# Holding early loads behind the first cache-page splits, moving the window-row copies into the mixer, and loading a table from another queue

## The chip, the cores and the metric

The kernel runs on one core of a Trainium2 chip. The core has five engines with instruction streams of their own: TensorE (PE in the profile; its weight loads are PEld), VectorE (DVE), ScalarE (ACT), GpSimd (POOL) and SyncE (SP). Its 16 DMA engines serve queues that SP and POOL issue into. The metric is the device time of one execution in microseconds (us); lower is better.

## The reference

One layer of a decoder trunk, in fp32, for 512 prompt tokens and 8 samples of 4 new tokens each (544 tokens in all), width 1024. Cut to what matters here:

```python
def layer(x, c, conv_prev, attend, w):
    mod = jax.nn.silu(c) @ w['w_ada'] + w['b_ada']          # modulation, 6 x 1024 columns
    sh1, sc1, g1, sh2, sc2, g2 = jnp.split(mod[:, None, :], 6, axis=-1)
    h = rmsnorm(x, w['norm1']) * (1 + sc1) + sh1
    bg, cg, xin, q, kc, vc, ks, vs, kw, vw, nsa_g, merge_g = split_columns(h @ w['w_in'])
    v, conv_new = short_conv(cg * xin, conv_prev, w['w_conv'], w['b_conv'])
    y_a = (bg * v) @ w['w_out_conv']
    ...
    o_b, nsa_state = attend(qh, gates, kvh(kc, vc), kvh(ks, vs), kvh(kw, vw))
    y_b = o_b @ w['w_o_nsa']
    ga, gb = jnp.split(jax.nn.sigmoid(merge_g), 2, axis=-1)
    x = x + g1 * ((ga * y_a + gb * y_b) @ w['w_out'])
    h2 = rmsnorm(x, w['norm2']) * (1 + sc2) + sh2
    x = x + g2 * ((jax.nn.silu(h2 @ w['w_gate']) * (h2 @ w['w_up'])) @ w['w_down'])

def compress(rows, pe, w1, w2):      # rows of the paged cache, for each sample 1024 past tokens
    ...
    return jax.nn.gelu(flat @ w1) @ w2

def nsa_sample(...):
    kc, vc = compress_kv(full_rows(cache_cmp, kv_cmp), pe, w1, w2)
    ...
    win = jnp.concatenate([cache_win, kv_win], axis=1)
    o = attend_block(q, gates, qpos, kc, vc, sel_t[0], sel_t[1], win[:, :, 0], win[:, :, 1], kwpos, slopes)
    return o, (kv_cmp, kv_sel, win[:, s:])      # new_win_sample: 508 old rows moved up by 4, then 4 new
```

So one output, `new_win_sample`, is mostly a shifted copy of an input: for each of the 8 samples rows 4 to 511 of `cache_win` go to rows 0 to 507, 1 MB per sample.

## The kernel before, in words

Every fp32 product is made of three matmuls. `split` (L213) takes a float tile apart into a high part (ACT, `wh`, L219) and a low part (DVE, `wl`, L220); `mm3` (L224 to L226) multiplies high by high, high by low and low by high. Weights come in slabs of 1 MB (`slab`, L207), each a DMA from SP's queue into one of three buffers named `raw`. The tokens stand in two halves of 288 and 256 columns. An accumulator of the linears is called `lin`.

The stages, in time of the profiled execution:

- 0 to 22 us: tables, the first compression weights (`phi_load`, `phi_split`), the first slab of modulation weights; TensorE also runs transposes of an identity matrix (`wake`, L514) that compute nothing.
- to 166 us: 16 units n = 0 to 15 that compress the cached rows of 8 samples (two units for each). `cmp_gather` (L448) issues 8 indirect DMAs from GpSimd, one for each 256 KB page of a sample; `cmp_split` (L470 on ACT, L471 on DVE) splits the pages into `xh` and `xl`; `cmp_M` (L483 to L485) runs 48 matmuls into `phi`. Between the units `mod_slab` (L273, `modp`) multiplies the eight modulation slabs, and the first normalisation of `xT` (the transposed input) is worked out: `square_acc`, the norm, `modulate`.
- to 306 us: key, value and query linears, whose results go to scratch memory (`q_dr`).
- to 543 us: the mixer. `conv_gen(k)` (three linears for each of eight column blocks; every second block loads three slabs `cg`, `xin`, `bg`) is interleaved with `sample_gen(bp)` for four pairs of samples: scores against compressed rows (`sx`, `px`), the choice of blocks (`imp`), then attention over gathered rows (`sraw`) and over the window rows (`wraw`, L899, two 1 MB DMAs from GpSimd), with transposes of the keys into `kt` (L842). The table `tb` (L716, 1 MB) holds distances and masks for it.
- to 1342 us: the convolution's output linear, prompt attention, output projection, FFN.

The order on each engine is set by a list scheduler of the tile framework, which works with estimated times, so that an instruction can stand far from where it is written. `tc.issue_after(ins)` keeps what is issued inside it behind `ins` on the engine of `ins`. `win_shift` is written in the FFN's loop, but its DMAs read an input and write an output and wait for nothing; the scheduler placed all eight much earlier, at 20.8, 87.1, 109.8, 143.6, 187.2, 220.5, 282.6 and 313.8 us on SP's queue. The loop it is written in:

```python
    for c2 in range(1, FC // 2):
        sg, su = slab("fg", c2), slab("fu", c2)
        if c2 <= DEC_B:
            win_shift(c2 - 1)
```

Of the kernel before, what the change touches and what calls it, by code (L numbers as in the profile page):

```python
# [9 lines left out]
F32 = mybir.dt.float32  # L10
F32R = mybir.dt.float32r
I32 = mybir.dt.int32
AF = mybir.ActivationFunctionType
# [6 lines left out]
KC = 8  # L20
# [5 lines left out]
DEC_B = 8  # L26
# [116 lines left out]
def build(tc, a, o):  # L143
# [58 lines left out]
    def raw_tile(n):  # L202
        return wpool.tile([128, 2048], F32, tag="raw", bufs=3, name=nm(n))

    last_slab = [None]

    def slab(*key):  # L207
        nk, ncol = len(SLABS[key][1]), len(SLABS[key][2])
        v = raw_tile("raw")[:, 0:nk * ncol]
        last_slab[0] = sync.dma_start(v, a["wt"][SLAB_AT[key], :, 0:nk * ncol])  # L210
        return v.rearrange("p (k f) -> p k f", k=nk)

# [49 lines left out]
    cT = cst.tile([128, 8, 32], F32, name="cT")  # L262
    pool.memset(cT, 0.0)

    last_m4 = [None]

    def mod_slab(s, v=None):
        v = slab("ada", s) if v is None else v
        p = tp_ps(nm("modp"))
        for k in range(KC):  # L270
            for hh in range(2):
                j = (k % 2) * 2 + hh
                pe.matmul(p[32 * j:32 * j + 32, 0:128], lhsT=cT[:, k, :], rhs=v[:, k, hh * 128:(hh + 1) * 128], start=(k < 2), stop=(k >= 6))  # L273
        m4 = wpool.tile([128, 128], F32, tag="m4", bufs=2, name=nm("m4"))
        last_m4[0] = act.activation(m4, p[:, 0:128], AF.Copy)
        if modp:
            modp.pop()()
        modp.append(lambda: mod_fin(s, m4))
# [178 lines left out]
    act.activation(cT[:, :, 0:9], c_in.rearrange("p (k n) -> p k n", k=8), AF.Silu)  # L457
    ada0 = slab("ada", 0)

    last_hi = [None]  # L460

    def cmp_split(b, v, hc):

        c0 = v * 256 + hc * 128
        hi = wpool.tile([128, 8, 128], F32R, tag=("wh", "wl")[hc], bufs=2, name=nm("xh"))
        lo = gat.tile([128, 8, 128], F32R, tag="xl", bufs=4, name=nm("xl"))
        n = 8 // len(gb_[b])
        for q, t in enumerate(gb_[b]):
            raw, js = t[:, :, c0:c0 + 128], slice(n * q, n * q + n)
            last_hi[0] = act.activation(hi[:, js], raw, AF.Copy)  # L470
            dve.tensor_sub(lo[:, js], raw, hi[:, js].bitcast(F32))  # L471
        return hi, lo

    def cmp_M(v, xs_, po):
# [35 lines left out]
    def wake(n):  # L510

        p = tp_ps(nm("wake"))
        for k in range(n):
            pe.transpose(p[:, (k % 4) * 128:(k % 4) * 128 + 128], ident, ident)  # L514
# [5 lines left out]
    phi_bias(0)  # L520
    cmp_gather(1)
    phi_load(1)
    sync.dma_start(xT.rearrange("p k n -> p (k n)"), a["xT"])
    mod_slab(0, ada0)
    wake(36)
    accs1 = [xp.tile([128, HW[hf]], F32, name=f"xacc{hf}") for hf in range(2)]
    fin_, mods = None, []
    with tc.issue_after(last_m4[0].ins):
        xs_ = [cmp_split(0, 0, hc) for hc in range(2)]
    cmp_gather(2)  # L530
    pool.memset(vext[32:64], 0.0)
    for n in range(16):
        b, v = n // 2, n % 2
        if n == 0:
            with tc.issue_after(last_hi[0].ins):
                for qt in range(4):
                    phi_split(1, qt)
        po = s_ps(nm("phi"))
        cmp_M(v, xs_, po)
        if fin_ is not None:  # L540
            fin_()
        fin_ = cmp_finish(b, v, po)
        if n < 15:
            xs_ = [cmp_split((n + 1) // 2, (n + 1) % 2, hc) for hc in range(2)]
        if n in (1, 3, 5, 8, 10):
            cmp_gather({1: 3, 3: 4, 5: 5, 8: 6, 10: 7}[n])
        if n == 0:
            phi_bias(1)
        if 0 < n < 8:
            mod_slab(n)  # L550
        if 2 <= n < 6:
            with tc.issue_after(last_hi[0].ins):
                for k in (2 * n - 4, 2 * n - 3):
                    for hf in range(2):
                        square_acc(xT, k, hf, accs1[hf], xp, k == 0)
        if n == 7:
            invs = [inv_bcast(inv_from_sums(tok_sums(accs1[hf], hf, xp), xp), hf, xp) for hf in range(2)]
        if n == 9:
            modp.pop()()
            make_A(n1T, sc1, A1)  # L560
            h = hh_, hl_ = tuple(hpool.tile([128, KC, NT], F32R, tag="h" + n_, bufs=1, name="h_" + n_) for n_ in "hl")
            mods = [modulate(xT, invs[hf], A1, sh1, hh_, hl_, hf, xp) for hf in range(2)]
        if 10 <= n < 14:
            for g_ in mods:
                for _ in range(2):
                    next(g_)
        if n == 13:
            mk8 = tsm[:, 19:27].rearrange("p (x m) -> p x m", x=1).broadcast_to([128, 8, 8])
            dve.tensor_mul(pm_.rearrange("p (b x) -> p b x", b=8), ptf.rearrange("p (b x) -> p b x", b=8), mk8)
            dve.tensor_reduce(fidx, pm_.rearrange("p (b x) -> p b x", b=8), axis=AX.X, op=ALU.add)  # L570
            dve.tensor_scalar(ixs, fidx, 16.0, tsm[:, 2:3], ALU.mult, ALU.add)
            xst.close()
# [140 lines left out]
    smp = mkpool(cst2, "smp", side="right")  # L713

    tb = smp.tile([128, TB_W], F32, name="tb")
    sync.dma_start(tb, a["tab_b"])  # L716
    off = 0
    tbs = []
    for w_ in (1024, 512, 64, 128, 16, 128, 128, 4):
# [10 lines left out]
    def conv_gen(k):  # L730
# [22 lines left out]
        def ev_b(hf, p):  # L753
# [4 lines left out]
                dve.tensor_mul(yinf[:, k, TS:288], p[:, TS:288], v[:, 0:256])  # L758
            else:
                dve.tensor_mul(yinf[:, k, 288:NT], p, v[:, 256:512])  # L760
        yield from linear_gen(split(slab_for("bg", k)[:, :, cs]), h, ev_b)

    def slab_for(nme, k):
        if k % 2 == 0:
# [539 lines left out]
    for hf in range(2):  # L1304
        for c, g_, w in early:
# [1 line left out]
            if hf == 0:  # L1307
                next(nh)
            ffn_up(c, g_, w[1], hf)
    def win_shift(b):  # L1310
        flat = lambda z: z.rearrange("t w -> (t w)").rearrange("(p f) -> p f", p=128)
        sync.dma_start(flat(o["new_win_sample"][b, 0:508, :]), flat(a["cache_win"][b, 4:512, :]))

    wxst.close()
    n2st.close()
    f6b = mkpool(f6st, "f6b", side="right")
# [1 line left out]
        ffn_tiles(f6b, c)  # L1318
    for c2 in range(1, FC // 2):
        sg, su = slab("fg", c2), slab("fu", c2)  # L1320
        if c2 <= DEC_B:
            win_shift(c2 - 1)
        for cc in range(2):
            c, g_ = c2 * 2 + cc, ffg()
            for v, fn in ((sg, lambda w, hf: ffn_gate(g_, w, hf)), (su, lambda w, hf: ffn_up(c, g_, w, hf))):
                w = split(v[:, :, cc * 128:cc * 128 + 128])
                for hf in range(2):
                    fn(w, hf)
# [119 lines left out]
```

## Time and profile before

| | |
|---|---|
| median of 3 runs | 1330.43 us (1330.1 to 1330.92) |
| profiled execution | 1343.92 us, its span 1342.1 us, mean granted TensorE clock 0.986 |
| TensorE busy | 1297.8 us, 97% of the span |
| DVE, ACT, POOL busy | 642.8, 540.4, 122.4 us |
| DMA | 191.37 MB, mean 143 GB/s |

A page of the profile is one execution. It lists busy time by engine, the span in 40 slices, the DMA queues, the chain of work that ended last and the costliest groups of instructions. In a group or in the timeline `out<-in` names what an instruction writes and reads, with partitions x elements; the bracket at a row's end is the engine's idle time just before and what ended it ("issue" is time in which the engine waited for nothing that the profile shows). The granted clock is the share of full speed that the throttle gave TensorE.

### The profile page before, as it was taken

To read this page: it belongs to the slowest core of one execution; us is meant where nothing else is said; L and a number is where in the kernel's file an instruction comes from. 1 tells how busy PE (TensorE), PEld (TensorE's weight loads), DVE (VectorE), ACT (ScalarE), POOL (GpSimd) and SP (SyncE) were. 2 spreads that over 40 slices of the span, in tenths; PEclk is the share of its full clock that TensorE was granted. 3 is DMA by queue.
4 is the path that set the end of the run, shared out by engine and by line. 5 is a ranking of instruction groups with operands and counts; after the bars stand their busy time and mean duration, and the time that the engine had idled before them with its cause. 6 is when DMAs were issued, how large, how long until landed. Compare 5 with 4: busy or idle time off the path is not lost.

```text
span 1342.1 us, 26018 instructions
## 1 busy us (share of the span) xinstructions
PE 1297.8 (97%) x11020; PEld 1216.4 (91%) x11020; DVE 642.8 (48%) x1554; ACT 540.4 (40%) x1068; POOL 122.4 (9%) x168
## 2 busy tenths in 40 slices
PE   4889999998999999999999999999999999999997
PEld 4879899998999999999777777999999999999997
DVE  1546732234454454525677676667433333333335
ACT  2545533423332334324776776435323223222223
POOL 5743130000011110001000000000000000000000
PEclk8989999998999999999999999999999999999998
DMA  9773426575435452743357235431112223122211
GB/s 369 240 244 123 153 101 230 200 241 174 188 129 194 178 224 95 193 134 131 115 159 201 95 116 189 143 126 64 63 63 96 94 68 122 56 87 87 87 64 67
DMA packets 37188, 191.37 MB, mean 143 GB/s; under 512 B 4780, under 2 KB 10284, under 8 KB 21584
## 3 DMA queue, kind: packets, MB, share of 16 engines
q1 hardware_dynamic: 29648, 147.77, 32.7%
q0 software_dynamic: 7424, 41.95, 8.8%
q8 instruction: 86, 1.41, 0.4%
q14 instruction: 30, 0.25, 0.1%
HBM read 174.49 MB, written 23.54 MB: 148 GB/s over the span
## 4 chain that ended last, share of the span: by engine, by line
PE 94%; DMA 2%; DVE 2%; issue 1%; ACT 1%; POOL 0%; another core or an unknown queue 0%; ACTq 0%; DVEq 0%
PE lin L224 19%; PE lin L225 19%; PE lin L226 19%; PE dn L226 3%; PE dn L224 3%; PE dn L225 3%; PE acc L1125 3%; PE ptp L1131 3%; PE phi L483 2%; PE phi L484 2%; PE phi L485 2%; PE modp L273 2%; DMA gt<-in_cache_cmp,ixc 2%; PE kt L842 2%; PE sp L1100 1%
## 5 line engine op out<-in xcount | busy, mean ns | idle before, releaser
L220 DVE TENSOR_TENSOR wl<-raw,wh 128x1024 fp32r<-128x1024 f32 (+1 forms) x148 | 178.7, 1208 | 284.2 <-ACT wh L219 277.8
L219 ACT ACTIVATE wh<-raw 128x1024 fp32r<-128x1024 f32 (+1 forms) x148 | 155.1, 1048 | 340.0 <-PE lin L225 248.3
L224 PE MATMUL lin<-h_h,wh 128*128 128x288 f32 x976 | 287.2, 294 | 0.0
L226 PE MATMUL lin<-h_h,wl 128*128 128x288 f32 x976 | 281.4, 288 | 0.0
L225 PE MATMUL lin<-h_l,wh 128*128 128x288 f32 x976 | 281.2, 288 | 0.0
L225 PE MATMUL lin<-h_lo,wh 128*128 128x288 f32 (+1 forms) x672 | 193.9, 289 | 0.0
L226 PE MATMUL lin<-h_hi,wl 128*128 128x288 f32 (+1 forms) x672 | 193.4, 289 | 0.0
L224 PEld LDWEIGHTS lin<-h_h,wh 128*128 128x128 f32 x976 | 184.2, 189 | 9.4 <-issue 8.1
L224 PE MATMUL lin<-h_hi,wh 128*128 128x288 f32 (+1 forms) x672 | 192.7, 287 | 0.0
L225 PEld LDWEIGHTS lin<-h_l,wh 128*128 128x128 f32 x976 | 184.1, 189 | 0.4
L226 PEld LDWEIGHTS lin<-h_h,wl 128*128 128x128 f32 x976 | 183.8, 188 | 0.3
L224 PEld LDWEIGHTS lin<-h_hi,wh 128*128 128x128 f32 x672 | 126.8, 189 | 0.0
L225 PEld LDWEIGHTS lin<-h_lo,wh 128*128 128x128 f32 x672 | 126.5, 189 | 0.2 <-DVE h_lo L349 0.2
L226 PEld LDWEIGHTS lin<-h_hi,wl 128*128 128x128 f32 x672 | 126.1, 188 | 0.0
L224 PE MATMUL dn<-f_hi,wh 128*128 128x256 f32 (+1 forms) x352 | 101.7, 289 | 0.0
L226 PE MATMUL dn<-f_hi,wl 128*128 128x256 f32 (+1 forms) x352 | 101.5, 288 | 0.0
L225 PE MATMUL dn<-f_lo,wh 128*128 128x256 f32 (+1 forms) x352 | 101.1, 287 | 0.0
L483 PE MATMUL phi<-xh,wph 128*128 128x256 f32 x256 | 75.8, 296 | 11.7 <-ACT xh L470 10.6
L1107 ACT ACTIVATE P<-P,nms 128x512 f32<-128x512 f32 (+3 forms) x128 | 70.8, 556 | 19.5 <-DVE nms L1106 18.5
L484 PE MATMUL phi<-xl,wph 128*128 128x256 f32 x256 | 74.6, 291 | 1.4 <-DVE xl L471 0.7
L448 POOL DMA_INDIRECT gt<-in_cache_cmp,ixc x64 | 69.1, 1080 | 65.8 <-DVE xl L471 23.8
L485 PE MATMUL phi<-xh,wpl 128*128 128x256 f32 x256 | 74.1, 289 | 0.8 <-issue 0.7
(350 smaller groups left out, 2450.1 us busy)
## 6 DMA issues: line engine op xcount, KB each, us to landing
raw<-in_wt SPq DMA_DIRECT2D x98, 1024.0 KB, 5.1
wraw<-in_cache_win POOLq DMA_DIRECT2D x8, 1024.0 KB
out_new_win_sample<-in_cache_win SPq DMA_DIRECT2D x8, 1016.0 KB, 9.4
raw<-in_wt SPq DMA_DIRECT2D x4, 768.0 KB
xT<-in_xT SPq DMA_DIRECT2D x1, 2176.0 KB
x<-in_xT SPq DMA_DIRECT2D x1, 2176.0 KB
gb<-gb_dr SPq DMA_DIRECT2D x8, 272.0 KB, 2.7
out_y_prompt<-ys SPq DMA_DIRECT2D x4, 512.0 KB
```

The lines of the kernel that those rows point to most:

```text
L219: act.activation(oh, view, AF.Copy)
L220: dve.tensor_sub(ol, view, oh.bitcast(F32))
L224: pe.matmul(p, lhsT=wh[:, k, :], rhs=xh, start=start, stop=False)
L225: pe.matmul(p, lhsT=wh[:, k, :], rhs=xl, start=False, stop=False)
L226: pe.matmul(p, lhsT=wl[:, k, :], rhs=xh, start=False, stop=stop)
L448: pool.indirect_dma_start(out=t, out_offset=None, in_=a["cache_cmp"], in_offset=bass.IndirectOffsetOnAxis(ap=ixc[:, col:col + 1], axis=0))
L483: pe.matmul(ps_, lhsT=w_h, rhs=mh, start=(ch == 0 and s == 0), stop=False)
L484: pe.matmul(ps_, lhsT=w_h, rhs=ml, start=False, stop=False)
L485: pe.matmul(ps_, lhsT=w_l, rhs=mh, start=False, stop=(ch == 7 and s == 1))
L1107: act.activation(t[:, 0:n], t[:, 0:n], AF.Exp, scale=-1.0, bias=nms[:, c:c + 1], accum_out=sums[:, c:c + 1])
L1125: pe.matmul(acc[br * 64:br * 64 + 64, :], lhsT=vtok[br][:, j, g * 64:(g + 1) * 64], rhs=pts_[br], start=(j == 0), stop=False)
L1131: pe.transpose(tp[:, r * 128:(r + 1) * 128], P[br, r][:, 128 * j:128 * j + 128], ident)
```

## The change

1. `mark(t, gate)` writes one element of a tile on DVE behind the instruction `gate`; a DMA into that tile waits for it. With it the slabs of modulation units 1 and 2 and `xT` are held behind low splits of the first cache pages.
2. The modulation slabs 1 to 7 are taken at units n = 1, 2, 4, 5, 7, 8, 10 instead of 1 to 7; squares at n = 5 to 8 instead of 2 to 5; the norm at 9 instead of 7; `modulate` from 11 on, in three pieces a unit (four in the last), instead of four pieces in units 10 to 13; page indices for the later gathers at 15 instead of 13.
3. The first `cmp_split` on ACT stands ahead of the copy out of `modp` of unit 0, no longer behind it.
4. `win_shift` stands in `conv_gen`, behind the last slab, as two DMAs of 64 and 63 blocks of 8 KB (even and odd blocks).
5. `tb` is loaded from GpSimd's queue.

```diff
+    def mark(t, gate):
+
+        with tc.issue_after(gate.ins):
+            dve.memset(t[0:1, 0:1], 0.0)
+
+    def slab(*key, gate=None):
         nk, ncol = len(SLABS[key][1]), len(SLABS[key][2])
         v = raw_tile("raw")[:, 0:nk * ncol]
+        if gate is not None:
+            mark(v, gate)
         last_slab[0] = sync.dma_start(v, a["wt"][SLAB_AT[key], :, 0:nk * ncol])
...
+    MODS = (1, 2, 4, 5, 7, 8, 10)
...
-            dve.tensor_sub(lo[:, js], raw, hi[:, js].bitcast(F32))
+            last_lo[0] = dve.tensor_sub(lo[:, js], raw, hi[:, js].bitcast(F32))
...
-    sync.dma_start(xT.rearrange("p k n -> p (k n)"), a["xT"])
-    mod_slab(0, ada0)
-    wake(36)
...
-    with tc.issue_after(last_m4[0].ins):
-        xs_ = [cmp_split(0, 0, hc) for hc in range(2)]
+    xs_ = [cmp_split(0, 0, hc) for hc in range(2)]
+    with tc.issue_after(last_hi[0].ins):
+        mod_slab(0, ada0)
+    wake(36)
...
+        if n < 3:
+            gate = last_lo[0]
         if n < 15:
             xs_ = [cmp_split((n + 1) // 2, (n + 1) % 2, hc) for hc in range(2)]
...
-        if 0 < n < 8:
-            mod_slab(n)
-        if 2 <= n < 6:
+        if n in MODS:
+            mod_slab(MODS.index(n) + 1, gate=gate if n < 3 else None)
+        if n == 2:
+            xTf = xT.rearrange("p k n -> p (k n)")
+            mark(xTf, gate)
+            sync.dma_start(xTf, a["xT"])
+        if 5 <= n < 9:
             with tc.issue_after(last_hi[0].ins):
-                for k in (2 * n - 4, 2 * n - 3):
+                for k in (2 * n - 10, 2 * n - 9):
...
-        if 10 <= n < 14:
-            for g_ in mods:
-                for _ in range(2):
-                    next(g_)
-        if n == 13:
+        for _ in range(3 if n < 15 else 4):
+            if units:
+                next(units.pop(0))
+        if n == 15:
...
     tb = smp.tile([128, TB_W], F32, name="tb")
-    sync.dma_start(tb, a["tab_b"])
+    pool.dma_start(tb, a["tab_b"])
...
-        yield from linear_gen(split(slab_for("bg", k)[:, :, cs]), h, ev_b)
+        bg = slab_for("bg", k)
+        win_shift(k)
+        yield from linear_gen(split(bg[:, :, cs]), h, ev_b)
+
+    def win_shift(b):
+
+        blocks = lambda z: z.rearrange("(n t) w -> n (t w)", t=4)
+        src, dst = blocks(a["cache_win"][b, 4:512, :]), blocks(o["new_win_sample"][b, 0:508, :])
+        with tc.issue_after(last_slab[0].ins):
+            for h_ in range(2):
+                last_slab[0] = sync.dma_start(dst[h_::2], src[h_::2])
...
-    def win_shift(b):
-        flat = lambda z: z.rearrange("t w -> (t w)").rearrange("(p f) -> p f", p=128)
-        sync.dma_start(flat(o["new_win_sample"][b, 0:508, :]), flat(a["cache_win"][b, 4:512, :]))
...
-        if c2 <= DEC_B:
-            win_shift(c2 - 1)
```

What this makes of the order on the engines, at the three places that matter. First SP's queue at the start (the `raw` tiles are slabs: in both the first two are compression weights, the third modulation slab 0). Before:

```order
L210 DMA raw_252<-in_wt 128x2048
L523 DMA xT<-in_xT 128x4352
L210 DMA raw_500<-in_wt 128x2048
L210 DMA raw_594<-in_wt 128x2048
L1312 DMA out_new_win_sample<-in_cache_win 16x16256
L210 DMA raw_703<-in_wt 128x2048
```

After:

```order
L217 DMA raw_252<-in_wt 128x2048
L217 DMA raw_499<-in_wt 128x2048
L217 DMA raw_767<-in_wt 128x2048
L217 DMA raw_594<-in_wt 128x2048
L563 DMA xT<-in_xT 128x4352
L217 DMA raw_868<-in_wt 128x2048
```

`xT` moved behind three slabs, of which the first (`raw_499`, modulation unit 1) and the third (`raw_594`, unit 2) are held by a mark, as `xT` is; the copy of window rows is gone from here.

Second, SP's queue in the mixer (`q_dr1h` and `q_dr1l` are the last query writes; `raw_4017`, `raw_4085` and `raw_4209` are the three slabs of the second pair of column blocks, in the change `raw_4024`, `raw_4092`, `raw_4216`). Before:

```order
L704 DMA q_dr1l<-ql_3345 128x512
L1312 DMA out_new_win_sample<-in_cache_win 16x16256
L716 DMA tb<-in_tab_b 128x2004
L725 DMA stT<-in_state_conv 128x128
L210 DMA raw_4017<-in_wt 128x2048
L210 DMA raw_4085<-in_wt 128x2048
L210 DMA raw_4209<-in_wt 128x2048
L210 DMA raw_4600<-in_wt 128x2048
```

After:

```order
L217 DMA raw_4024<-in_wt 128x2048
L217 DMA raw_4092<-in_wt 128x2048
L217 DMA raw_4216<-in_wt 128x2048
L783 DMA out_new_win_sample<-in_cache_win 64x2048
L783 DMA out_new_win_sample<-in_cache_win 63x2048
L783 DMA out_new_win_sample<-in_cache_win 64x2048
L783 DMA out_new_win_sample<-in_cache_win 63x2048
L217 DMA raw_4611<-in_wt 128x2048
```

The copies of two samples now follow the third slab; the same stands at the next two pairs of column blocks, and the first two copies stand among the query writes. On GpSimd's queue `tb` now stands right behind the second gather of the first pair.

Third, DVE at the first pair of samples (`up` is written from the two halves of the `xin` linear, `lin_3519` and `lin_3546` before, `lin_3522` and `lin_3549` after; `wl_3741` is the low split for a later linear). Before:

```order
L742 TENSOR_TENSOR up_3510<-lin_3519,cg_3424 128x256
L744 TENSOR_TENSOR up_3510<-lin_3546,cg_3424 128x256
L220 TENSOR_TENSOR wl_3741<-raw_3425,wh_3740 128x1024
L793 TENSOR_TENSOR gm_3487<-tb,gT 48x128
L771 ISA sxs_3498,n_404_3500<-sx_3489,tb 128x63
```

After:

```order
L754 TENSOR_TENSOR up_3513<-lin_3522,cg_3427 128x256
L815 TENSOR_TENSOR gm_3490<-tb,gT 48x128
L793 ISA sxs_3501,n_404_3503<-sx_3492,tb 128x63
L793 ISA n_404_3503 128x1
L793 ISA sxs_3501,n_404_3503<-sx_3492,tb 128x32
L793 ISA n_404_3503 128x1
L793 ISA sxs_3501,n_404_3503<-sx_3492,tb 128x32
L793 ISA n_404_3503 128x1
L890 COPY nx_3583<-n_404_3503 128x1
L756 TENSOR_TENSOR up_3513<-lin_3549,cg_3427 128x256
L832 RECIPROCAL rc_3510<-sm_3507 128x1
L833 TENSOR_SCALAR px_3502<-px_3502,rc_3510 128x63
```

The readers of `tb` (`gm`, the score pieces `sxs`) moved ahead of the second `up`, and the low split went behind `px` and the first steps on `imp`.

More of the change, by code (lines that the diff above doesn't have):

```diff
@@ L205, in build @@
     last_slab = [None]
-    def slab(*key):
+    def mark(t, gate):
+        with tc.issue_after(gate.ins):
+            dve.memset(t[0:1, 0:1], 0.0)
+    def slab(*key, gate=None):
         nk, ncol = len(SLABS[key][1]), len(SLABS[key][2])
         v = raw_tile("raw")[:, 0:nk * ncol]
+        if gate is not None:
+            mark(v, gate)
         last_slab[0] = sync.dma_start(v, a["wt"][SLAB_AT[key], :, 0:nk * ncol])
@@ L263, in build, with mod_slab @@
     pool.memset(cT, 0.0)
-    last_m4 = [None]
-    def mod_slab(s, v=None):
-        v = slab("ada", s) if v is None else v
+    MODS = (1, 2, 4, 5, 7, 8, 10)
+    def mod_slab(s, v=None, gate=None):
+        v = slab("ada", s, gate=gate) if v is None else v
         p = tp_ps(nm("modp"))
@@ L274, in mod_slab @@
         m4 = wpool.tile([128, 128], F32, tag="m4", bufs=2, name=nm("m4"))
-        last_m4[0] = act.activation(m4, p[:, 0:128], AF.Copy)
+        act.activation(m4, p[:, 0:128], AF.Copy)
         if modp:
@@ L458, in build @@
     ada0 = slab("ada", 0)
-    last_hi = [None]
+    last_hi, last_lo = [None], [None]
     def cmp_split(b, v, hc):
@@ L522, in build @@
     phi_load(1)
-    sync.dma_start(xT.rearrange("p k n -> p (k n)"), a["xT"])
-    mod_slab(0, ada0)
-    wake(36)
     accs1 = [xp.tile([128, HW[hf]], F32, name=f"xacc{hf}") for hf in range(2)]
     fin_, mods = None, []
-    with tc.issue_after(last_m4[0].ins):
-        xs_ = [cmp_split(0, 0, hc) for hc in range(2)]
+    xs_ = [cmp_split(0, 0, hc) for hc in range(2)]
+    with tc.issue_after(last_hi[0].ins):
+        mod_slab(0, ada0)
+    wake(36)
     cmp_gather(2)
     pool.memset(vext[32:64], 0.0)
+    units = []
     for n in range(16):
@@ L548, in build @@
             phi_bias(1)
-        if 0 < n < 8:
-            mod_slab(n)
-        if 2 <= n < 6:
+        if n in MODS:
[5 more added lines that the diff above has]
+        if 5 <= n < 9:
             with tc.issue_after(last_hi[0].ins):
-                for k in (2 * n - 4, 2 * n - 3):
+                for k in (2 * n - 10, 2 * n - 9):
                     for hf in range(2):
                         square_acc(xT, k, hf, accs1[hf], xp, k == 0)
-        if n == 7:
+        if n == 9:
             invs = [inv_bcast(inv_from_sums(tok_sums(accs1[hf], hf, xp), xp), hf, xp) for hf in range(2)]
-        if n == 9:
+        if n == 11:
             modp.pop()()
@@ L561, in build @@
             h = hh_, hl_ = tuple(hpool.tile([128, KC, NT], F32R, tag="h" + n_, bufs=1, name="h_" + n_) for n_ in "hl")
-            mods = [modulate(xT, invs[hf], A1, sh1, hh_, hl_, hf, xp) for hf in range(2)]
-        if 10 <= n < 14:
-            for g_ in mods:
-                for _ in range(2):
-                    next(g_)
-        if n == 13:
+            units = [u for hf in range(2) for u in [modulate(xT, invs[hf], A1, sh1, hh_, hl_, hf, xp)] * KC]
+        for _ in range(3 if n < 15 else 4):
+            if units:
+                next(units.pop(0))
+        if n == 15:
             mk8 = tsm[:, 19:27].rearrange("p (x m) -> p x m", x=1).broadcast_to([128, 8, 8])
```

## The prediction

> **What bounds the kernel now.** I read the page first: the span, the busy shares and the chain of work that ended last.
>
> ```profile
> span 1342.1 us, 26018 instructions
> PE 1297.8 (97%) x11020; PEld 1216.4 (91%) x11020; DVE 642.8 (48%) x1554; ACT 540.4 (40%) x1068; POOL 122.4 (9%) x168
> PE 94%; DMA 2%; DVE 2%; issue 1%; ACT 1%; POOL 0%; another core or an unknown queue 0%; ACTq 0%; DVEq 0%
> ```
>
> TensorE is the bound: busy for 97%, and 94% of the chain. The change takes no matmul away, so it can only win in TensorE's idle 44 us and in stretches at a low granted clock. Next come TensorE's waits, longest first (line, what it waited for, us in total, times, longest).
>
> ```profile
> PE phi L483 <- ACT xh L470: 10.6, 1, 10.6
> PE imp L814 <- DVE px L811: 3.6, 1, 3.6
> PE modp L273 <- issue: 3.0, 6, 1.0
> ```
>
> The first two are single stalls, and the change touches both. So I read the timeline at each.
>
> **The start.** Columns: start, duration, engine, line, operation; in brackets the idle time before and what ended it.
>
> ```profile
> 14.01 0.95 POOL L448 DMA_INDIRECT gt<-in_cache_cmp,ixc  x1 [0.30 <-issue]
> 20.31 1.91 PE L514 MATMUL wake<-ident 128*128 128x128 f32 x16 [0.43 <-issue]
> 31.73 2.00 ACT L470 ACTIVATE xh<-gt 128x1024 fp32r<-128x1024 f32 x2 [11.03 <-DMA gt<-in_cache_cmp,ixc]
> 32.82 2.36 DVE L471 TENSOR_TENSOR xl<-gt,xh 128x1024 fp32r<-128x1024 f32 x2 [18.71 <-DMA gt<-in_cache_cmp,ixc]
> 32.84 0.58 PE L483 MATMUL phi<-xh,wph 128*128 128x256 f32 x1 [10.62 <-ACT xh L470]
> 34.10 0.58 PE L484 MATMUL phi<-xl,wph 128*128 128x256 f32 x1 [0.68 <-DVE xl L471]
> ```
>
> TensorE ends its setup at 20.31 + 1.91 = 22.22 and stands until 32.84, because the first gather of cache pages lands only at 31.7. ACT splits it then, and the first phi matmul follows. The gather's last page (the eighth row of its kind, the one at 14.01) was issued by 15. What it waited behind, in the DMA view of 2 to 31.7 us (issues, KB each, median us to landing):
>
> ```profile
> DMA packets 2182, 11.67 MB, mean 393 GB/s; under 512 B 434, under 2 KB 690, under 8 KB 1397
> raw<-in_wt SPq DMA_DIRECT2D x5, 1024.0 KB, 8.3
> xT<-in_xT SPq DMA_DIRECT2D x1, 2176.0 KB
> out_new_win_sample<-in_cache_win SPq DMA_DIRECT2D x1, 1016.0 KB
> gt<-in_cache_cmp,ixc POOLq DMA_INDIRECT x15
> gb<-gb_dr SPq DMA_DIRECT2D x8, 272.0 KB, 2.7
> ```
>
> (The last row is the page's, for the landing time of a small load.) The engines are full at 393 GB/s. The change takes out of this stretch xT (2.23 MB), the two slabs of modulation units 1 and 2 (2.10) and one copy of window rows (1.04): 5.37 MB, or 13.7 us at that rate. Gather 0 would land at 31.7 - 13.7 = 18.0. Its own queue sets a second bound: last page issued by 15.0, plus 2.7 for a load of such a size, is 17.7. I take 18.0. The split then needs 32.84 - 31.73 = 1.1 us for xh and 34.10 - 31.73 = 2.4 for xl, which is ready at 20.4, ahead of 22.2. So phi starts at about 22.3: 32.84 - 22.3 = 10.5 us, and the 0.68 us wait for xl goes too.
>
> The clock comes on top. Stretches (window, its length, busy us and counts of PE, PEld, DVE, ACT, POOL; granted clock; DMA share; GB/s):
>
> ```profile
> 32.84:38.20 5.36, 4.68 (x20) 4.39 (x21) 5.36 (x7) 4.88 (x7) 4.15 (x4) 0.50 0.75 245
> 82.70:89.60 6.90, 5.21 (x24) 4.38 (x25) 3.44 (x9) 1.84 (x5) 2.98 (x2) 0.51 0.83 294
> 325.10:331.90 6.80, 5.77 (x25) 5.66 (x26) 4.84 (x20) 2.38 (x5) 1.44 (x4) 0.50 0.45 154
> 120.00:165.00 45.00, 43.42 (x363) 40.94 (x362) 34.29 (x79) 25.71 (x51) 9.29 (x9) 1.00 0.34 118
> ```
>
> After the stall TensorE runs 5.36 us at clock 0.50; without the 0.68 us wait that is 4.7 us of work, of which half, 2.3, comes back if phi follows the setup without a pause. The start's term: 10.5 + 0.7 + 2.3 = **13.5 us**. The Trainium skill (TensorE: Matmul & The Clock Gate, Part 1) lets full rate return after one busy window of some 3.4 us, which would make the clock part an estimated 1.7 and the term 12.9. This trace shows 4.7 to 6.9 us at half rate after three stalls, so the row decides.
>
> Held-back loads come with dates to keep:
>
> ```profile
> 37.56 2.35 DVE L471 TENSOR_TENSOR xl<-gt,xh 128x1024 fp32r<-128x1024 f32 x2
> 45.83 1.22 DVE L471 TENSOR_TENSOR xl<-gt,xh 128x1024 fp32r<-128x1024 f32 x1
> 52.03 1.08 PE L273 MATMUL modp<-raw,cT 128*32 128x128 f32 x32
> 62.23 1.08 PE L273 MATMUL modp<-raw,cT 128*32 128x128 f32 x32
> raw<-in_wt SPq DMA_DIRECT2D x98, 1024.0 KB, 5.1
> ```
>
> The first two rows end with the splits behind which the slabs of modulation units 1 and 2 are now held (39.9 and 47.1 before), the next two are these units. With everything 13.5 earlier the slab of unit 1 is let go at 26.4, lands 5.1 (the last row) to 8.3 us later, at 31.5 to 34.7, and is needed at 38.5. That of unit 2 is let go at 33.6, lands by 45 even behind another slab, and is needed at 48.7. xT follows it, and its first squares now stand at n = 5, three phi units further on, and 52.03 to 62.23 shows one to be 9 us long here. Behind these held DMAs SP's queue has only later slabs. One date is tight: the slab of the sixth modulation unit gets its buffer only when unit 5 is done, one phi unit before its own use. A unit's 48 matmuls take 6 us at the rate of the row 120 to 165 above (363 in 45 us), 7 with a modp; the slab takes 5.1 to 8.3: 0 to 1.5 us lost. I take 0, since by then the copies and xT are out of the way and 5.1, the median, fits.
>
> The squares, the norm and modulate only move within the phi stage. The row 120 to 165 has DVE at 34.29 of 45 us and ACT at 25.71 under a full TensorE, and modulate now spreads over five units instead of four: nothing, and if that cover went, a part of the 10.7 us that DVE has left there would be overrun. The three one-element memsets (at most 0.26 us each, what a 63-column row of DVE takes further down) and eight more DMA issues on SP (at most tb's 1.28 us each) lie beside TensorE.
>
> **The table tb.** The second stall, with TensorE's last linear matmul of that place first:
>
> ```profile
> 322.22 0.28 PE L226 MATMUL lin<-h_h,wl 128*128 128x256 f32 x1
> 322.61 0.42 DVE L744 TENSOR_TENSOR up<-lin,cg 128x256 f32<-128x256 f32 x1 [2.31 <-PE lin L226]
> 323.51 1.23 DVE L220 TENSOR_TENSOR wl<-raw,wh 128x1024 fp32r<-128x1024 f32 x1 [0.48 <-ACT wh L219]
> 324.65 0.28 DVE L793 TENSOR_TENSOR gm<-tb,gT 48x128 f32<-48x128 f32 x1
> 325.78 0.26 DVE L811 TENSOR_SCALAR px<-px,rc 128x63 f32<-128x63 f32 x1
> 326.13 0.66 PE L814 MATMUL imp<-px,tb 128*128 128x64 f32 x2 [3.64 <-DVE px L811]
> 314.39 1.28 SPq L716 DMA_DIRECT2D tb<-in_tab_b  x1
> 235.82 0.97 POOL L781 DMA_INDIRECT sraw<-in_cache_sel,ixs  x1 [0.54 <-ACT vext L628]
> ```
>
> DVE idles ahead of up, yet gm and the softmax pieces behind it, which read tb, come after up and after the split wl, that waits for ACT. tb was issued at 314.39, so the scheduler set its readers late. In the change tb's DMA stands right behind the gather at 235.82, and gm and the softmax's first part stand ahead of the second up; the split wl goes behind. When lin ends (322.5) there remain up from 322.61 on (0.42), the reciprocal (under px's 0.26) and the 0.35 from px's start to imp's: imp starts near 323.6, 2.5 us earlier. With a pause so short the half-rate stretch 325.10:331.90 should go: from imp at 326.13 on it is 5.8 us, half of it 2.9. Term: **5.4 us**. The split that now comes later feeds a linear beyond the key transposes and the linear now under way, and DVE is busy for 4.84 us of the 6.80 there. On GpSimd nothing of this stage stands behind tb that TensorE awaits.
>
> The Trainium skill (DMA: Bandwidth & Descriptors, Issuing engines are not separate DMA queues) says that another issuing engine only saves the sequencer's time to start the DMA. Taken alone that would be 1.28 us of SP, off the path, and the sum 5.4 us smaller. Here the order changes as well, which the rule doesn't cover; no run shows it yet.
>
> **The window copies.** Eight copies, two of them now in each of four places. They gave no wait of TensorE before except at the start, counted above. New is what they meet:
>
> ```profile
> 324.76 26.25 SPq L210 DMA_DIRECT2D raw<-in_wt  x3
> 350.60 1.14 POOL L899 DMA_DIRECT2D wraw<-in_cache_win  x2 [17.78 <-PE sacc L892]
> 361.83 0.93 PE L842 MATMUL kt<-ident,wraw 128*128 128x128 f32 x7
> out_new_win_sample<-in_cache_win SPq DMA_DIRECT2D x8, 1016.0 KB, 9.4
> DMA packets 580, 5.28 MB, mean 330 GB/s; under 512 B 66, under 2 KB 66, under 8 KB 66
> ```
>
> (The last row is the DMA view of 350 to 366.) Copies of two samples now follow the third slab, issued at 351.0, just as wraw (2.1 MB) is issued at 350.6 and needed in two halves, the second at 361.83. Two copies alone take 18.8 us. If the two queues share the engines equally, 2.1 MB of wraw beside 2.1 of copies, 4.2 + 1.05 for the slab at 393 GB/s = 13.6 us, wraw ends at 364.2, 2.4 late. At the other end it costs nothing, if wraw's packets stand first, or a whole copy, 9.4, if the copies do. I take **-2.4**, the equal share. In the later pairs the copies again follow the third slab; I cost them at nothing, hidden by linears, and at up to 9.4 each in a rival. The first two copies, by the q writes, meet only slabs issued ahead.
>
> **Sum.** 13.5 + 5.4 - 2.4 = 16.5 us. The profiled execution took 1343.92 us (span 1342.1), 13.5 above the median of the runs, 1330.43. 1343.92 - 16.5 = 1327.4; on the median 1330.4 - 16.5 = **1314**.
>
> **Rivals.**
> - Slower: the copies, in front of wraw, hold it in each of three pairs for a whole copy, 3 x 9.4 = 28.2 against 18.9 won: 1330.4 + 9.3 = 1340. It decides from 6.3 us a pair. For it: copy and wraw share engines that the row 350 to 366 shows at 330 GB/s. Against: before, no wait for wraw stands among TensorE's, and with an equal share even the tightest pair loses 2.4. Chance 7%.
> - Held slabs come late at modulation units 1, 2 and 6, with landings of 13 us rather than 8: some 5 us, and half-rate stretches again, 2.5: 1314 + 7.5 = 1321. For it: full engines at that time. 12%.
> - The gather isn't freed: its own queue, and not the other loads, sets its landing at some 25, midway between 18 and 31.7, and only half the start is won: 1314 + 7 = 1321 to 1322. 8%.
> - The readers of tb come no earlier, because DVE still ends up first and something else there is late: 1314 + 5.4 = 1319. For it: up, behind the last lin, stays ahead of px. 10%.
> - More goes than I count: with copies out of the phi stage the other issue waits for modp (3.0 us) and the half-rate stretch 82.70:89.60 (5.21 busy, 2.6 back) go, and wraw isn't late: 1314 - 3.0 - 2.6 - 2.4 = 1306. For it: the stretch has DMA at 0.83. 15%.
> - No change beyond what a measurement of this kernel can tell (0.2% each way, 2.7 us): gains and collisions cancel. 5%.
>
> The forecast keeps 43%, within 1310 to 1317.5. The range 1304 to 1324 holds all but the first and last rival and a little of the tails. Slower by over 0.2%: 7%; within: 6%; faster: 87%.
>
> **What would show it.** Right: first phi near 22.3 at clock 1.00; imp with an idle time near 1; the kt of the first wraw pair late by 0 to 3 us, later ones on time; modp with no DMA wait. Wrong: gather 0 landing beyond 22, a raw DMA named ahead of modp, wraw named ahead of kt in more than one pair, or the half clock still there after imp.

## The result and the profile after

| | before | after | predicted |
|---|---|---|---|
| median | 1330.68 us (4 runs, 1330.1 to 1331.23) | 1320.76 us (4 runs, 1319.52 to 1323.1) | 1314 (1304 to 1324) |
| ratio | 1 | 0.9928, 95% interval 0.991 to 0.9945 | 0.988 |
| profiled execution | 1343.92 us | 1319.79 us | |

The change wins 9.9 us of the 16.5 forecast; the median after lies within 1304 to 1324, and outside the 1310 to 1317.5 that the prediction gave to the forecast itself. The sizes of two of its three terms held, one of them for another reason than the prediction gave, and two things are given back that it left out. On another chip, where the kernel before takes 1345 us, the changed kernel is slower (1.0066); on a third, where before takes 1347, the variant nearest to it is slower too. The later experiments ran on these two.

The page after: span, busy shares and the chain that ended last.

```profile
span 1318.0 us, 26044 instructions
PE 1290.8 (98%) x11020; PEld 1212.7 (92%) x11020; DVE 641.2 (49%) x1557; ACT 540.2 (41%) x1068; POOL 126.5 (10%) x169
PE 93%; DMA 3%; DVE 2%; POOL 1%; issue 1%; ACT 1%; SPq 0%; ACTq 0%; DVEq 0%
```

TensorE's waits after, those that the change bears on (line, what it waited for, us in total, times, longest):

```profile
PE pbt L437 <- DVE pbs L435: 6.2, 2, 3.3
PE kt L864 <- DMA wraw<-in_cache_win: 3.0, 2, 2.3
PE imp L836 <- POOL ncv L762: 1.0, 1, 1.0
PE modp L280 <- DMA raw<-in_wt: 0.5, 1, 0.5
```

The wait of 10.6 us for `xh` is gone and the one ahead of `imp` fell from 3.6 to 1.0. A second wait for `pbs` and the waits for `wraw` are new. The timeline at the start, after:

```profile
14.98 5.96 PE L521 MATMUL wake<-ident 128*128 128x128 f32 x36
19.20 2.01 ACT L477 ACTIVATE xh<-gt 128x1024 fp32r<-128x1024 f32 x2 [7.75 <-DMA gt<-in_cache_cmp,ixc]
20.70 0.36 PE L490 MATMUL phi<-xh,wph 128*128 128x256 f32 x1
21.57 0.39 PE L491 MATMUL phi<-xl,wph 128*128 128x256 f32 x1 [0.51 <-DVE xl L478]
```

Gather 0 lands at 19.2 instead of 31.7, and phi follows the transposes without a pause.

The trace of before that the prediction read took 13 us more than that kernel's runs. So the accounts below start from a second trace of it (the first experiment).

### The profile page after: what moved, and what is told of

It reads as the page before. It is cut to its first block, busy times and chain, and to the rows that moved or that the text cites. A ratio compares the mean times of both kernels' runs of the same rounds, so it can differ in the third digit from the quotient of the medians.

```text
span 1318.0 us, 26044 instructions
## 1 busy us (share of the span) xinstructions
PE 1290.8 (98%) x11020; PEld 1212.7 (92%) x11020; DVE 641.2 (49%) x1557; ACT 540.2 (41%) x1068; POOL 126.5 (10%) x169
## 4 chain that ended last, share of the span: by engine, by line
PE 93%; DMA 3%; DVE 2%; POOL 1%; issue 1%; ACT 1%; SPq 0%; ACTq 0%; DVEq 0%
PE lin L231 19%; PE lin L232 19%; PE lin L233 19%; PE dn L233 3%; PE dn L231 3%; PE dn L232 3%; PE acc L1147 3%; PE ptp L1153 3%; PE phi L490 2%; PE phi L491 2%; PE phi L492 2%; PE modp L280 2%; DMA wraw<-in_cache_win 2%; PE kt L864 2%; POOL gt L455 1%; PE sp L1122 1%
## 5 line engine op out<-in xcount | busy, mean ns | idle before, releaser
L455 POOL DMA_INDIRECT gt<-in_cache_cmp,ixc x64 | 72.5, 1134 | 35.4 <-issue 17.2
```

Of the source, the lines that this page charges most:

```text
L455: pool.indirect_dma_start(out=t, out_offset=None, in_=a["cache_cmp"], in_offset=bass.IndirectOffsetOnAxis(ap=ixc[:, col:col + 1], axis=0))
```

## The experiments

**The kernel before, a second and a third time.** No edit.

> The kernel before, unchanged, profiled a second time. Between the two profiled executions the changed kernel is 24.1 us shorter (1343.92 to 1319.79), between the medians 9.9. Theory A (the traces as they stand are typical): the second profile again has a span near 1342, with a stall of some 10 us ahead of the first phi and half-rate stretches at 71 to 90 us. Theory B (the first profile of before was a slow draw of the same kernel, 13 us of it in the first 166 us): a span near 1329, with the stall ahead of phi shorter, or the loss at 71 to 90 us gone.

> The kernel before, unchanged, for its trace where it takes some 1345 and not 1330. In the traces of the changed kernel phi starts at 20.7 us where before takes 1330, but near 40 where before takes 1345, behind 23 us of issue waits. Theory A (instructions arrive late while gathers fill the DMA engines, and before hides that behind its own wait for gather 0): phi starts at 33 to 36 in before, with 4 to 10 us of issue waits ahead of it and the wait for the gather shortened by as much, and more issue waits among the modulation units up to 100 us. Theory B (before is slower there for another reason): no issue waits, phi at 32.8. If before takes 1330 in this call, it shows nothing new.

Measured: 1330.83 us (span 1329.1) and 1328.87 (span 1327.1). The waits of TensorE in the second trace of before:

```profile
PE phi L483 <- ACT xh L470: 12.0, 1, 12.0
PE imp L814 <- DVE px L811: 3.6, 1, 3.6
PE pbt L430 <- DVE pbs L428: 2.5, 1, 2.5
```

Theory B holds in part: the first trace was not typical of the kernel, but the stall ahead of phi is not shorter here, it is even longer. What is missing is the half-rate stretch at 82.7 (the clock there is 1.00 now) and the waits for issue: 3.0 us at `modp` and others in the first trace, the longest of them this:

```profile
PE pbt L430 <- issue: 4.3, 1, 4.3
```

It is longer than the wait ahead of `imp`, and the prediction's list of waits, longest first, leaves it out. The second trace lists no wait for issue. The rival by which more goes than counted had 5.6 of its 8 us from these waits and that stretch: in an ordinary execution that part was not there to win. The third trace stands like the second (phi at 32.8, no wait for issue listed), so its question stays open: there is no trace of before from a chip where it takes 1345.

Set matmul by matmul against the trace of after (the n-th of each kind against the n-th), this second trace gives the account of the change. After is ahead by 12.1 us at the first phi and by 14.7 at the end of the first unit; by 9.7 half a unit later; by 10.2 ahead of `imp` in the mixer, 15.8 behind it; by 11.0 behind the second `wraw`, and so to the end (spans 1329.1 and 1318.0).

**tb's queue alone.**

```diff
-    sync.dma_start(tb, a["tab_b"])
+    pool.dma_start(tb, a["tab_b"])
```

> Only tb's load goes to GpSimd's queue; loads at the start and window copies stand as before. By the prediction's term (the stall ahead of imp falls from 3.64 to about 1 us and the half-rate stretch behind it goes) 5.4 us less than before, ratio 0.996. Rival: another queue only saves SP's 1.28 us beside TensorE's work, ratio 1.000, imp waiting as long as before.

Measured: 1331.09, ratio 1.0003 (0.9994 to 1.0012), and 3.3 us of wait ahead of `imp`. The profile names no cause for it, but the last step that `imp` needs, `px`, ends at 314.6 and `imp` starts at 314.7. VectorE, then ScalarE, there:

```profile
309.08 0.27 DVE L793 TENSOR_TENSOR gm<-tb,gT 48x128 f32<-48x128 f32 x1
311.47 0.43 DVE L744 TENSOR_TENSOR up<-lin,cg 128x256 f32<-128x256 f32 x1 [1.75 <-PE lin L226]
312.37 1.22 DVE L220 TENSOR_TENSOR wl<-raw,wh 128x1024 fp32r<-128x1024 f32 x1 [0.42 <-ACT wh L219]
314.12 0.16 DVE L810 RECIPROCAL rc<-sm 128x1 f32<-128x1 f32 x1 [0.53 <-ACT px L808]
311.28 1.06 ACT L219 ACTIVATE wh<-raw 128x1024 fp32r<-128x1024 f32 x1 [4.95 <-PE lin L225]
313.65 0.35 ACT L808 ACTIVATE px<-sxs,n 128x63 f32<-128x63 f32 x1
```

`gm` moved ahead of the second `up`, as in the change, but the split `wh` and `wl` still stands ahead of the exponential and the reciprocal on both engines. Moving some of the readers is not enough. The Trainium skill (DMA: Bandwidth & Descriptors, Issuing engines are not separate DMA queues) had it so: another engine to issue saves only the time of issuing. This run agrees.

**The copies out of the way, in the kernel before.** They keep their form and are held behind the FFN's slabs.

```diff
-        sync.dma_start(flat(o["new_win_sample"][b, 0:508, :]), flat(a["cache_win"][b, 4:512, :]))
+        with tc.issue_after(last_slab[0].ins):
+            last_slab[0] = sync.dma_start(flat(o["new_win_sample"][b, 0:508, :]), flat(a["cache_win"][b, 4:512, :]))
```

> The kernel before with only the window copies moved: each stays one DMA of 16 rows of 65 KB but is held behind the slabs of the FFN's loop, so that none is left at the start, in the phi stage, the linears or the mixer. The start loses one copy of 1.04 MB from its 11.67 MB, 2.7 us at 393 GB/s; the copy at 87 us leaves the phi stage. In this order tb's readers on DVE also stand ahead of the second up, so the stall ahead of imp should shorten by 2.5 us, 5.4 with the half-rate stretch. Theory A: 8 us less than before, ratio 0.994. Rival: copies far from TensorE's waits cost nothing and the order is nothing, ratio 1.000.

Measured: 1342.95, ratio 1.0087 (1.0072 to 1.0103). A miss in the sum, not in the part: the wait ahead of `imp` fell to 0.7 us, with tb on SP's queue, while six waits for `wh` turned up in the FFN:

```profile
PE lin L224 <- ACT wh L219: 11.5, 6, 1.9
PE imp L814 <- POOL ncv L750: 0.7, 1, 0.7
```

VectorE, then TensorE, at `imp`:

```profile
305.85 0.29 DVE L793 TENSOR_TENSOR gm<-tb,gT 48x128 f32<-48x128 f32 x1
308.24 0.42 DVE L744 TENSOR_TENSOR up<-lin,cg 128x256 f32<-128x256 f32 x1 [1.28 <-PE lin L226]
308.58 0.24 DVE L811 TENSOR_SCALAR px<-px,rc 128x63 f32<-128x63 f32 x1
309.27 1.23 DVE L220 TENSOR_TENSOR wl<-raw,wh 128x1024 fp32r<-128x1024 f32 x1 [0.45 <-ACT wh L219]
308.93 0.41 PE L814 MATMUL imp<-px,tb 128*128 128x64 f32 x2 [0.72 <-POOL ncv L750]
```

Here `gm` stands ahead of the second `up` and the split `wl` behind `px`, as in the change, and the copies alone were moved. Matmul by matmul against the second trace of before, this kernel is ahead by 2.2 us at the first phi (gather 0 lands at 29.5 instead of 31.7), by 1.0 ahead of `imp` and by 6.9 behind it. In the FFN it then loses 20 us.

SP, ScalarE and TensorE at the first of the waits for `wh`:

```profile
994.88 22.67 SPq L210 DMA_DIRECT2D raw<-in_wt  x2
1002.39 0.45 ACT L254 ACTIVATE f_hi<-ffg 128x288 fp32r<-128x288 f32 x1 [3.37 <-DVE ffg L1276]
1005.14 0.42 ACT L254 ACTIVATE f_hi<-ffg 128x256 fp32r<-128x256 f32 x1 [2.30 <-DVE ffg L1276]
1005.46 1.99 ACT L219 ACTIVATE wh<-raw 128x1024 fp32r<-128x1024 f32 x2
1006.55 0.40 PE L224 MATMUL lin<-h_hi,wh 128*128 128x288 f32 x1 [1.91 <-ACT wh L219]
```

The slab was issued at 994.9 and landed at 999.8. ScalarE idles ahead of both `f_hi` and takes the split at 1005.46 without a pause behind them: the split is late because it stands behind `f_hi`, not because its slab is.

**The copies out of the way, in the changed kernel.** The 8 KB blocks stay; `win_shift` is called in the FFN's loop.

```diff
-        bg = slab_for("bg", k)
-        win_shift(k)
-        yield from linear_gen(split(bg[:, :, cs]), h, ev_b)
+        yield from linear_gen(split(slab_for("bg", k)[:, :, cs]), h, ev_b)
...
         sg, su = slab("fg", c2), slab("fu", c2)
+        if c2 <= DEC_B:
+            win_shift(c2 - 1)
```

> The changed kernel with the window copies (same 8 KB blocks) held behind the slabs of the FFN's loop instead of the mixer's. If the copies hold wraw up in the mixer (waits of 2.3 and 0.7 us ahead of kt in the trace of after, and 9 us at a clock of 0.81 behind the first), those waits go: 4.8 us less than the changed kernel, 1316, ratio to before 0.989. Rival: wraw is late by the slabs and gathers beside it and not by the copies, 1321, ratio 0.993, with the waits still there. If eight copies in the FFN collide with its slabs, it is slower than the changed kernel and the FFN shows waits for raw.

Measured: 1314.78, ratio 0.9892 (0.9877 to 0.9908), as expected: some 6 us less than the changed kernel, and the fastest of all. The mixer's waits for `wraw` in the timeline of after:

```profile
335.48 1.29 PE L864 MATMUL kt<-ident,wraw 128*128 128x128 f32 x8 [2.32 <-DMA wraw<-in_cache_win]
391.39 0.85 PE L864 MATMUL kt<-ident,wraw 128*128 128x128 f32 x6 [0.66 <-DMA wraw<-in_cache_win]
```

The stretch behind the first, in after and then with the copies in the FFN (window, length, busy us and counts of PE, PEld, DVE, ACT, POOL; granted clock; DMA share; GB/s):

```profile
333.00:342.00 9.00, 6.68 (x42) 5.40 (x41) 2.50 (x5) 1.65 (x2) 0.00 (x0) 0.81 0.81 343
```

```profile
333.00:342.00 9.00, 9.00 (x74) 8.03 (x73) 4.14 (x11) 3.21 (x8) 0.00 (x0) 1.00 0.21 89
```

With the copies gone from the mixer no wait for `wraw` is left and the clock is full. So both are the copies' doing: 2.3 + 0.7 + 9 x 0.19 = 4.7 us. Matmul by matmul after falls back by 4.9 us against this kernel, from `imp` to behind the second `wraw`.

**The same with 65 KB rows.** As the last, but one DMA of 16 rows for each sample.

```diff
-            for h_ in range(2):
-                last_slab[0] = sync.dma_start(dst[h_::2], src[h_::2])
+            last_slab[0] = sync.dma_start(flat(o["new_win_sample"][b, 0:508, :]), flat(a["cache_win"][b, 4:512, :]))
```

> The changed kernel with the window copies behind the FFN's slabs, in the old form: one DMA of 16 rows of 65 KB for each sample, not 127 blocks of 8 KB. The same place with 8 KB blocks took 1314.8 and showed no wait of TensorE in the FFN. If the block size sets what a copy costs the slabs behind it, six waits of 1.9 and 0.5 us with half-rate stretches come, some 19 us: 1334, ratio 1.003. Rival: the block size is nothing, and the kernel before with copies in the FFN lost its time otherwise: 1315, ratio 0.988.

Measured on a chip where before took 1347.24: 1368.12, ratio 1.0166 (1.013 to 1.0201). The kernel with the bias steps first (below) has its copies in 8 KB blocks at this place and took 1352.2 on the same chip, so the form costs some 16 us. Matmul by matmul between these two traces it is 19.5 us in the FFN, since the order of the bias steps makes a difference at the start as well. Its waits:

```profile
PE lin L231 <- ACT wh L226: 11.5, 6, 1.9
PE lin L233 <- DVE wl L227: 2.1, 5, 0.5
```

Six waits of the same size stood in the kernel before with the copies in the FFN. The size of the effect agrees with the theory in the expectation, its mechanism does not: no wait for a slab shows. With the form of the copy the place changes at which the scheduler puts the split on ScalarE. That it expects a longer copy with 65 KB rows is argued from these orders; its estimates were not looked at.

**tb back on SP's queue, in the changed kernel.**

```diff
-    pool.dma_start(tb, a["tab_b"])
+    sync.dma_start(tb, a["tab_b"])
```

> The changed kernel with tb loaded from SP's queue again, between the third and the fourth DMA of the first two window copies; gm and the scores still stand ahead of the second up. The load of tb from GpSimd alone gave 1.0003 of before with the wait ahead of imp unchanged, so my theory now is that the early copies' place in SP's queue, and not tb's queue, sets that order and the wait: as the changed kernel, 1320.8, ratio to before 0.993, wait ahead of imp about 1 us. The prediction's step (tb's queue wins 5.4 us): 1326, ratio 0.997.

Measured where before took 1347.24: 1356.69, ratio 1.0072 (1.0046 to 1.0098). Against before that says nothing on the expectation, since the changed kernel itself stands at 1.0066 on such a chip (below). Against that figure, from another chip, tb's queue is worth nothing that shows, and the wait is the one of after, 1.0 us:

```profile
PE imp L836 <- POOL ncv L762: 1.0, 1, 1.0
```

**The marks taken out.** As the kernel with its copies in the FFN, without the three marks.

```diff
-            mark(v, gate)
+            pass
...
-            mark(xTf, gate)
```

> The changed kernel with copies behind the FFN's slabs in 8 KB blocks (1314.8), without the three marks: xT and the slabs of modulation units 1 and 2 load as soon as they can. If holding them is what frees gather 0, 4.3 MB (11 us at 393 GB/s) stand beside it again and phi starts near 30: the stall of 9 to 10 us and a half-rate stretch come back, 1325, ratio 0.996. Rival: the early copy alone had delayed the gather, or the gather's own queue sets its landing: 1315 to 1318, ratio 0.989 to 0.991.

Measured where before took 1347.24: 1344.46, ratio 0.9982 (0.9962 to 1.0002). ScalarE's first split of gather 0, here and then with the marks (the kernel of the next experiment, on the same chip, its copies in the FFN as well):

```profile
27.76 2.00 ACT L477 ACTIVATE xh<-gt 128x1024 fp32r<-128x1024 f32 x2 [16.41 <-DMA gt<-in_cache_cmp,ixc]
18.12 2.00 ACT L479 ACTIVATE xh<-gt 128x1024 fp32r<-128x1024 f32 x2 [6.85 <-DMA gt<-in_cache_cmp,ixc]
```

In the two other kernels with marks that ran on this chip the split starts at 17.9 and 18.0. So the marks bring gather 0 forward by 9.6 us, and the first theory of the expectation is right on the gather: without them phi starts at 28.9. It is wrong on the time. With the marks TensorE waits for issue on this chip, and phi starts only at 42.6, so the kernel without them is the faster one there; its own wait for `xh` is no more than 4.0 us, because it too waits for issue first (6.5 us ahead of `pbt`). What the marks are worth in time where before takes 1330 was not measured.

**The bias steps ahead of the second gather's splits.** In after, VectorE and ScalarE do this while TensorE waits for `pbs`:

```profile
29.48 1.06 ACT L477 ACTIVATE xh<-gt 128x1024 fp32r<-128x1024 f32 x1 [4.14 <-DMA gt<-in_cache_cmp,ixc]
30.44 0.46 ACT L498 ACTIVATE t<-phi,pbias 128x256 f32<-128x256 f32 x1
30.57 1.23 DVE L478 TENSOR_TENSOR xl<-gt,xh 128x1024 fp32r<-128x1024 f32 x1 [3.19 <-ACT xh L477]
32.12 0.28 DVE L435 COPY pbs<-pb 128x128 f32<-128x128 f32 x1
32.45 0.59 PE L437 MATMUL pbt<-sel,pbs 128*128 128x1 f32 x2 [3.29 <-DVE pbs L435]
```

And the stretch behind it (columns as above):

```profile
32.45:38.20 5.75, 5.75 (x35) 5.75 (x36) 1.40 (x5) 2.59 (x3) 4.49 (x6) 0.71 1.01 418
```

Both engines stand before the split of gather 1, which lands at 29.4; `t` and `pbs` are queued behind it, and `pbt` on TensorE behind `pbs`. In the kernel with its copies in the FFN the split starts at 27.84, 1.6 us earlier, and the wait is 1.7 us shorter:

```profile
30.82 0.38 PE L437 MATMUL pbt<-sel,pbs 128*128 128x1 f32 x2 [1.59 <-DVE pbs L435]
```

The edit holds the split back, on top of the kernel with its copies in the FFN:

```diff
+        if n == 1:
+            with tc.issue_after(pbs_[0].ins), tc.issue_after(pbs_[1].ins):     # the copy to pbs, the first t
+                xs_ = [cmp_split(1, 0, hc) for hc in range(2)]
```

> The changed kernel with copies behind the FFN's slabs (1314.8), and the first splits of the second gather held on ACT and DVE behind the first unit's bias steps (t and pbs), so that the late gather no longer blocks them. In the trace of after TensorE waited 3.3 us for pbs, which stood on DVE behind the split of gather 1, and ran at a clock of 0.71 after it. If that order is the cause, the wait goes: 3 to 4 us less, 1311, ratio 0.9855. Rival: the gather is late anyway, and the wait turns up at the third unit's first phi: 1315, ratio 0.989.

> The same kernel as e3_bias_first (copies behind the FFN's slabs, first splits of the second gather held behind the bias steps), to be set against the changed kernel in the same call. If before takes 1330 again: 1311, ratio 0.9855, no wait for pbs. If 1347: some 1352, ratio 1.003, with the issue waits; the changed kernel then 5 us above it, for wraw.

Measured: 1352.2, ratio 1.0029 (1.001 to 1.0048), and 1351.61, ratio 1.0033 (1.0015 to 1.0051). Inconclusive for its question, since both were on chips where another wait rules the start. That the order behind the second gather costs the 5.0 us given back there is read from the trace of after, and the wait moving with the gather's date bears it out; no edit shows it.

**The changed kernel on another chip.** No edit.

> The changed kernel, once more. Its gain was 0.9928 where the kernel before took 1330.7; in the last call of four kernels before took 1347.2 and TensorE waited for issue (no instruction at hand) by 7 to 10 us ahead of pbt and by 10 to 14 us among the wake transposes, while gathers filled the DMA engines. Theory A: what sets the ratio is whether TensorE's instructions arrive late while the DMA engines are full; with before at 1330 it is 0.993 again, with before at 1347 it is 1.00 to 1.01, with issue waits ahead of phi. Theory B: the ratio doesn't depend on that and is 0.993 in both.

Measured: 1354.74 where before took 1345.2 (1339.01 to 1354.76), ratio 1.0066 (1.0043 to 1.009): slower. It came as theory A had it. TensorE, from the end of the first bias matmuls to the first phi:

```profile
21.08 0.58 PE L437 MATMUL pbt<-sel,pbs 128*128 128x1 f32 x2 [10.82 <-issue]
25.68 0.37 PE L521 MATMUL wake<-ident 128*128 128x128 f32 x1 [1.76 <-issue]
...
38.27 0.37 PE L521 MATMUL wake<-ident 128*128 128x128 f32 x1 [1.03 <-issue]
38.98 5.61 PE L521 MATMUL wake<-ident 128*128 128x128 f32 x28 [0.34 <-issue]
44.35 0.37 PE L490 MATMUL phi<-xh,wph 128*128 128x256 f32 x1
```

The profile names nothing that TensorE waits for: 10.8 us ahead of `pbt`, then 1 to 2.3 us ahead of single transposes. I take it that its next instruction is not there yet; the profile doesn't show that. Gather 0 is not late (its first split starts at 18.1), yet phi starts at 44.4 instead of 20.7. The DMA engines, in 40 slices of 2 to 42 us:

```profile
DMA  3999999999999997766787658775886957710000
```

They are busy until about 38, with the 24 pages of three gathers one behind the other, and TensorE's matmuls follow each other again from 39. In the first trace of before, which has such waits too but shorter ones, phi starts at 32.84, 11.5 us earlier. That the spans differ by 11.5 as well (1342.1 and 1353.6) is partly chance: matmul by matmul this lead is 8.5 at the end of the first unit, 11.4 at the first linear, 6.9 behind `imp` and 11.5 again behind the second `wraw`. `ib`, a step of the normalisation, waits another 3.4 us in this trace, and in none of before. I read the start so: without xT and the slabs beside them the gathers run ahead, at the price of TensorE's instructions. No trace of before on such a chip shows it.

**The third gather held, in the kernel with the bias steps first.**

```diff
-    cmp_gather(2)
+    cmp_gather(2, gate=last_lo[0])      # marks the tile of its first page
```

> As e4_bias_first, and the third gather (8 pages, 2.1 MB) held by a mark behind the first unit's xl splits. If full DMA engines keep TensorE's instructions away, the engines are empty some 5 us earlier ahead of phi (7.3 MB instead of 9.4): where before takes 1347, the issue waits among the wake transposes shrink by 5 us or more and the time falls to 1340 to 1347; where before takes 1330, nothing, 1311. Rival: instructions arrive late for another reason, and only the third gather's landing moves: no change of the issue waits, and up to 5 us more at unit 4.

Measured on the same chip: 1349.15, ratio 1.0018 (0.9992 to 1.0044), beside 1.0033 without the hold. The profiled execution was the shortest of its runs (1338.59); TensorE's wait in it, and the DMA engines' 40 slices of 2 to 42 us:

```profile
26.59 0.59 PE L439 MATMUL pbt<-sel,pbs 128*128 128x1 f32 x2 [16.56 <-issue]
```

```profile
DMA  3989999999999999867865875000003784979999
```

There the engines are empty from 27 to 32 us, and TensorE resumes at 26.6. None of the waits among the transposes is left (14.6 us in the kernel without the hold), but the one ahead of `pbt` grew from 7.2 to 16.6: in all 5.2 us less. That fits traffic as the cause. But full engines alone don't do it, for when the third gather runs they are full again, and TensorE stays busy (columns as above):

```profile
36.00:42.00 6.00, 5.85 (x60) 5.22 (x58) 0.00 (x0) 0.00 (x0) 4.74 (x6) 1.00 1.00 372
```

The other runs of this kernel took 1340 to 1354, so the hold wins nothing that the intervals show. What keeps the instructions away stays open: the trace shows one instruction load in the first 42 us, and not what it waited for.

## Why the prediction was right or wrong

- **The start, 13.5 us: right, and then partly given back.** Gather 0 landed at 19.2 (18.0 forecast), phi started at 20.7 (22.3) at a clock of 1.00, and after was ahead by 14.7 us at the end of the first unit. The mechanism is shown in two parts: moving the copies alone brought gather 0 forward by 2.2 us, and the marks, on another chip, by 9.6; of 12.5 in all.
- **The step that failed: the dates of the held-back loads.** They were worked out for the modulation slabs and xT, which kept them but for one wait of 0.5 us for `raw`, small, though the prediction had named it as a sign of being wrong. The second gather was not among them, though with phi 12 us earlier it is what is late next. An estimate from the prediction's own rows would have dated it: gather 0's last page is issued by 15.0, eight more pages follow 1.25 us apart, and 2.7 us for landing makes 27.7. It lands at 29.4, in time for its own unit, but its split stands in ScalarE's and VectorE's order ahead of `t` and `pbs`. That cost 3.3 us of wait and a low clock, 5.75 x 0.29 = 1.7 us: the 5.0 us between 14.7 and 9.7. The Trainium skill (TensorE: Matmul & The Clock Gate, Part 1) has full rate back after a busy window of 3.4 us. A clock of 0.71 over 5.75 us is an estimated 3.3 us at half rate, which agrees here, while the stretches after stalls quoted in the prediction ran on for 4.7 us and more.
- **imp, 5.4 us: the size right, the cause wrong.** After gained 5.6 us there (10.2 to 15.8), and by the steps forecast: the readers of tb ahead of the second `up`, the split behind `px`. But it was moving the copies that brought this order, not tb's queue: tb alone gave 1.0003, the copies alone brought 5.8 us (1.0 to 6.9) and a wait of 0.7, and without tb's move the changed kernel still waits 1.0. The prediction gave the gain to the part that names tb, though the order printed for the whole change doesn't say which part moved the rows. That the copies' move stood in the same change, and the 5.4 us came all the same, was luck. Why the scheduler orders them so was not looked at.
- **The copies, -2.4 us: mis-sized, they cost 4.7.** Equal sharing forecast the first wait well (2.3 measured, 2.4 forecast; its 5.25 MB at 393 GB/s are 13.4 us and not 13.6, so its own sum gives 2.1). The term lacked the low clock behind it (1.7), and the second pair, costed at nothing, lost 0.7: `wraw` named in a second pair was another of the prediction's signs of being wrong.
- **The sum.** 14.7 - 5.0 + 5.6 - 4.7 = 10.6 of the 11.1 us between the traces; 9.9 between the medians. The forecast of 16.5 was too high by the second gather (5.0) and the copies (2.3), and too low by 1.2 at the start.
- **The profile it started from.** Its execution lay 13.5 us above the median; the prediction said so and went on. The difference is the waits for issue, of which the prediction listed only those at `modp`, and the low clock around them. The stall that the start's term rests on was typical all the same (10.6 us; 12.0 and 10.7 in the later traces).

## What to carry to other kernels

When a wait is taken away at the front of a pipeline, date every transfer that follows, and look for what stands behind its consumer in the in-order queues: the late gather hurt a small copy a few rows down, not its own matmuls. Where a scheduler orders engines by estimates, moving a DMA or changing its form reorders instructions far away, so each part of an edit is to be ordered and timed by itself before a gain is put down to one of them. And if a profiled execution is 1% above the runs, find out why first: waits of the same kind stood in the traces from the chips where the change lost.

## What the runs showed of the hardware

- The kernel before took 1329 to 1332 us on some chips and 1339 to 1355 on two others, and the change went from 0.9928 to 1.0066. In the traces of its variants there TensorE stands for up to 16.6 us at a time without a cause that the profile names, while gathers keep the DMA engines busy. In the two traces shown, it goes on within 1 us of the end of that traffic; but engines just as full later in the start (372 GB/s) came with no such wait. Each of these chips was seen once, and the cause is open.
- Copies of 2 MB beside 2 MB of `wraw` held its second half up by 2.3 us, near what an equal share of the engines gives (2.1 to 2.4).
